# Regrouping the opening phase of a two-layer GLA and pooling kernel: stages of two tiles that carry keys and half of the values, each half of a modulation as one run

## The chip, the cores and the metric

The kernel runs on one core of one Trainium2 chip. The metric is the device time of one execution in microseconds (us), lower is better. Engines are named as in the profile: PE is TensorE's matmul side and PEld its weight load, DVE is VectorE, ACT is ScalarE, POOL is GpSimd, SP is the queue from which most transfers are started.

## What is computed

One batch of 256 rows of width 2048 (`x`) passes through two layers; 256 more rows (`ctx`) serve the first layer only. All tensors are float32.

```
for i in 0, 1:
    sh, sc, gt = split(silu(c) @ w_ada[i] + b_ada[i], 3)          # the modulation
    u = x * (1 + sc) + sh
    layer 0: uc = ctx * (1 + sc_c) + sh_c                         # same weights, condition c_ctx
             k, v, rf, rb of uc -> two final states s_f, s_b      # w_in_e columns of keys, values, ranks
             h = u @ w_in_e                                       # keys, values, ranks, queries, gates, convolution inputs
             y = concat(gla(h, s_f, s_b) * silu(gate), conv(h)) @ w_out_e
    layer 1: h = u @ w_in_o;  y = (pool(h) * silu(gate)) @ w_out_o
    x = layer_norm(alpha * x + gt * y, ln_g[i], ln_b[i])
```

The change concerns only the start of layer 0: the modulation's shift and scale for `x` and `ctx`, the modulated inputs `u` and `uc`, and their products with the key and value columns of `w_in_e`.

## The kernel before

**Products.** A float32 product is done as three matmuls in the type fp32r: both operands are split into a rounded part h and a rest l, and `mm3` issues uh*wh, uh*wl and ul*wh (L190 to L192), 512 columns each. A weight unit arrives in a `raw` buffer (four buffers of 1 MB, `load_unit`, L138, from the SP queue); `split_unit` makes the parts: a copy on ACT (L152), a subtraction on DVE (L153). The buffer is free when both are done. The list `specs` holds the weight units in the order of use, `w_ahead(nl, ns)` loads up to nl and splits up to ns units from the one in use on, `w_next` hands out the next.

**Opening phase.** The contraction of 2048 is cut into 16 tiles of 128. A stage takes one or two of them (`STAGES`: 1, 1, then seven times 2). `stage_u` makes the modulated input of its tiles. `mod_rows` loads the modulation weights of these columns, first the scale half, then the shift half, in units of 1 MB: for two tiles two units a half, for one tile one. Each unit is used by 8 or 16 products in four column strips of the array (L274, tile `ada`; float32 shows as two instructions a product), all into one bank `ps`. `to_cols` copies the bank (`arow`, ACT, L285) and turns it to columns (`adaT`, L288); `add_bias` finishes scale and shift (`modT`). Then the input tiles are transposed (`px`, L390 and L391), scaled on ACT and DVE (`u`), and split (`uxh`, `uxl` for `x`, `uch`, `ucl` for `ctx`). After every fourth tile four products in four strips add to the ranks (`pr`, L406, two instructions each).

`stage_k` multiplies a stage's tiles with the two halves of the key columns: for each half four groups (two row blocks of `x`, two of `ctx`) of 3 matmuls a tile, so 24 matmuls for two tiles; each group's bank is added to `knat` on DVE (L426; the first stage copies on ACT). `v_fill` does the same for one half of the value columns (tile `vfill`, added to `vnat`). `FILLS` places it for tiles 0 to 7 only. What is left of the values, tiles 8 to 15 of the first half and all of the second, is done behind the opening phase by `gemm` in quads of four tiles (tile `vacc`), after the keys are transposed (`nT`).

**Order.** The program text calls `stage_u` of a stage ahead of `stage_k` of the stage before it. A planner at build time then fixes each engine's order: an instruction with a lower priority number (by default its place in the text; `prio` shifts it) goes first when its inputs are there by the planner's own estimates. `issue_after` makes instructions of a block follow a given one on their engine. Engines run their order strictly, and `raw` buffers are given out in the order of the text.

**Background.** The other modulation columns are worked off on DVE, in units of 1 MB that are also `raw` buffers (`ada_accum`, L534, four instructions of 128x512 a unit). `pump_ada` starts them: none in the opening phase, then three per quad of values (`ADA_V`), and fewer later. The GLA's gate and score work is started by a budget at the same ticks, of 4500 a quad of values and 3000 a quad later.

Of the kernel before, what the change touches and what calls it, by code (L numbers as in the profile page):

```python
# [2 lines left out]

# [6 lines left out]
F32 = mybir.dt.float32  # L10
# [3 lines left out]
ALU = mybir.AluOpType  # L14
# [3 lines left out]
P = 128  # L18
D = 2048
KT = D // P  # L20
# [9 lines left out]
UF_ACT = 1  # L30
KRAW = False
GW_AT = 12
ADA_0 = {}
ADA_ORDER = "cgh"
ADA_O = 1
ADA_PRIO = 0
# [17 lines left out]
B_X = 3000  # L54
LA_SPLIT = 1
JG = 4
STAGES = (1, 1, 2, 2, 2, 2, 2, 2, 2)


@with_exitstack  # L60
def kernel(
# [47 lines left out]
    def const(shape, dt, name):  # L109
        return cpool.tile(shape, dt, tag=name, name=name)  # L110
# [77 lines left out]
    def mm3(acc, u, w, start, stop):  # L188
        (uh, ul), (wh, wl) = u, w
        nc.tensor.matmul(out=acc, lhsT=uh, rhs=wh, start=start, stop=False)  # L190
        nc.tensor.matmul(out=acc, lhsT=uh, rhs=wl, start=False, stop=False)  # L191
        nc.tensor.matmul(out=acc, lhsT=ul, rhs=wh, start=False, stop=stop)  # L192


    rows0 = slot([32, P], F32, "rows0")
# [29 lines left out]
    nc.gpsimd.dma_start(rows2[8:24, :], as_rows(pool_scale[0]))  # L225
    nc.gpsimd.dma_start(rows2[24:26, :], as_rows(gla_norm_w[0]))

    sel4 = const([P, 4], F32, "sel4")
    nc.vector.tensor_reduce(out=sel4, in_=ident.rearrange("p (g v) -> p v g", g=4)[:, 0:4, :], axis=AX.X, op=ALU.add)

# [29 lines left out]
    nc.gpsimd.dma_start(wr, w_in_e[0][:, D : D + 32].rearrange("(k p) n -> p k n", p=P))  # L260


    def mod_rows(k0, n):

        nw = n * P
        ps = mp([P, nw], "ada")
        nk = 2048 // nw
        for half, c0 in ((0, D + k0 * P), (1, k0 * P)):
            for kk in range(0, KT, nk):
                r = load_unit(w_ada[0], kk, nk, c0, nw)  # L270
                for j in range(nk):
                    kt = kk + j
                    g = kt % 4
                    nc.tensor.matmul(  # L274
                        out=ps[32 * g : 32 * g + 32, :], lhsT=sil[:, kt, 2 - 2 * half : 34 - 2 * half], rhs=r[:, j, :],
                        start=half == 0 and kt < 4, stop=half == 1 and kt >= KT - 4,
                    )
        return ps

    arow_ins = []  # L280

    def to_cols(ps, nw):
        n = nw // P
# [79 lines left out]

    quad_u = []

    def stage_u(k0, n):
        w, n0 = n * P, k0 * P
        xc = xcs.pop(k0, None)
        if xc is None:
            xc = load_xc(k0, n)  # L370
        xs, cs = xc[:, 0:2, :], xc[:, 2:4, :]
        ps = mod_rows(k0, n)
        if k0 == 0:
            cols_0()
        if k0 == 4:
            cols_1()
        if k0 == GW_AT:
            gate_weights()
        pt = to_cols(ps, w)
        ks = slice(k0, k0 + n)  # L380
        add_bias(scT[:, ks, :], pt[:, :, 0:2], bT[0][:, 16 + k0 : 16 + k0 + n].unsqueeze(2).to_broadcast([P, n, 2]), True)
        add_bias(shT[:, ks, :], pt[:, :, 2:4], bT[0][:, ks].unsqueeze(2).to_broadcast([P, n, 2]), False)
        for j in range(n):
            kt = k0 + j
            if kt % 2 == 0:
                quad_u.append(slot([P, 2, 512], F32, "u"))
            u = quad_u[-1]
            px = mp([P, 512], "px")
            for t in range(2):
                nc.tensor.transpose(out=px[:, t * P : (t + 1) * P], in_=xs[:, t, j * P : (j + 1) * P], identity=ident)  # L390
                nc.tensor.transpose(out=px[:, 256 + t * P : 256 + (t + 1) * P], in_=cs[:, t, j * P : (j + 1) * P], identity=ident)  # L391
# [7 lines left out]
            nc.scalar.copy(uch[q][:, i, :], uc)  # L399
            nc.vector.tensor_tensor(out=uxl[q][:, i, :], in0=ux, in1=uxh[q][:, i, :].bitcast(F32), op=ALU.subtract)  # L400
            nc.vector.tensor_tensor(out=ucl[q][:, i, :], in0=uc, in1=uch[q][:, i, :].bitcast(F32), op=ALU.subtract)
            if i == 3:
                pr = mp([P, 512], "pr")
                for g in range(4):
                    kk = kt - 3 + g
                    nc.tensor.matmul(  # L406
                        out=pr[32 * g : 32 * g + 32, :], lhsT=wr[:, kk, :], rhs=quad_u[kk // 2][:, kk % 2, :],
                        start=True, stop=True,
                    )
                if q == 0:  # L410
                    nc.vector.tensor_copy(r_acc, pr)
                else:
                    nc.vector.tensor_tensor(out=r_acc, in0=pr, in1=r_acc, op=ALU.add)

    def stage_k(k0, n):
        for nb in range(2):
            parts = w_next((W_E, k0, n, nb * 512), 0, 0)
            for m in range(4):
                acc = acc_bank("kacc")
                for j in range(n):  # L420
                    mm3(acc, utile(m, k0 + j), parts[j], j == 0, j == n - 1)
# [18 lines left out]

    vnat = []

    def v_fill(nb, kt, nk):

        parts = w_next((W_E, kt, nk, 1024 + nb * 512), 0, 0)
        if not vnat:
# [1 line left out]
        with prio(FILL_PRIO):  # L448
            for m in range(4):
                acc = acc_bank("vfill")  # L450
                for j in range(nk):
                    mm3(acc, utile(m, kt + j), parts[j], j == 0, j == nk - 1)
# [110 lines left out]
    }  # L563
    ada_bg.extend(jobs[n]() for n in ADA_ORDER)

    prev, k0 = None, 0
    for n in STAGES:
        if prev:
            w_ahead(2, SPLIT_0)
        stage_u(k0, n)  # L570
        if prev:
            stage_k(*prev)
            pump_ada(ADA_0.get(sum(prev), 0))
            for f in FILLS.get(sum(prev), ()):
                v_fill(*f)
        elif SPLIT_0:
            with tc.issue_after(arow_ins[0].ins):
                w_ahead(2, 2)
        prev = (k0, n)
        k0 += n  # L580
    n0_done[0] = True
    w_ahead(4, 2)
    stage_k(*prev)


    bg = []
# [801 lines left out]
```

## Time and profile before

| | us |
|---|---|
| Median of 3 runs (lowest, highest) | 1006.15 (1005.88, 1007.38) |
| Profiled execution, its own time | 1010.29 |
| Profiled execution, span of the trace | 1008.5 |
| First matmul of the keys starts (from the span's start) | 17.09 |
| Last `nT` transposes done, first `vacc` matmul starts | 198.91 |

The profile describes one execution. An engine's busy time is the time in which it had an instruction, a wait is the idle time ahead of an instruction with what ended it. Matmuls overlap, so the pace of PE is read from the distance of two starts and not from the duration of one matmul.

### The profile page before, as it was taken

To read this page: it belongs to the slowest core of one execution; us is meant where nothing else is said; L and a number is where in the kernel's file an instruction comes from. 1 tells how busy PE (TensorE), PEld (TensorE's weight loads), DVE (VectorE), ACT (ScalarE), POOL (GpSimd) and SP (SyncE) were. 2 spreads that over 40 slices of the span, in tenths; PEclk is the share of its full clock that TensorE was granted. 3 is DMA by queue.
4 is the path that set the end of the run, shared out by engine and by line. 5 is a ranking of instruction groups with operands and counts; after the bars stand their busy time and mean duration, and the time that the engine had idled before them with its cause. 6 is when DMAs were issued, how large, how long until landed. Compare 5 with 4: busy or idle time off the path is not lost.

```text
span 1008.5 us, 14323 instructions
## 1 busy us (share of the span) xinstructions
PE 960.9 (95%) x5654; PEld 759.2 (75%) x5654; DVE 801.6 (79%) x1142; ACT 469.3 (47%) x643; POOL 24.4 (2%) x56
## 2 busy tenths in 40 slices
PE   5899999999999999999999899999999999989995
PEld 4566656778878877887878778888778778778885
DVE  1555546979996999779999688897979997666676
ACT  2422214356675676236454344445745555435340
POOL 2000000000000000000000000000010001000000
PEclk9999999999999999999999999999999999999998
DMA  9977889566787586867767877985497999875532
GB/s 265 329 263 262 276 284 336 193 243 231 258 302 252 188 269 219 257 206 274 241 228 234 284 255 247 353 298 207 152 368 275 304 334 322 278 266 203 174 119 83
DMA packets 150371, 255.44 MB, mean 253 GB/s; under 512 B 5078, under 2 KB 46720, under 8 KB 150304
## 3 DMA queue, kind: packets, MB, share of 16 engines
q1 hardware_dynamic: 146592, 245.13, 72.4%
q0 software_dynamic: 2896, 8.72, 2.7%
q10 hardware_dynamic: 816, 0.68, 0.3%
q8 instruction: 44, 0.72, 0.3%
q14 instruction: 23, 0.19, 0.0%
HBM read 252.41 MB, written 2.10 MB: 252 GB/s over the span
## 4 chain that ended last, share of the span: by engine, by line
PE 41%; DVE 33%; DMA 18%; issue 5%; ACT 3%; SPq 0%; DVEq 0%; ACTq 0%
DMA raw<-in_w_ada_dram 15%; DVE wl L153 11%; DVE aacc L534 9%; PE oacc L191 5%; PE oacc L192 5%; PE oacc L190 5%; DMA raw<-in_w_in_o_dram 3%; PE xacc L192 3%; PE xacc L191 3%; PE xacc L190 3%; PE ada L274 2%; PE kacc L190 2%; PE kacc L192 2%; PE kacc L191 2%; PE pr L406 1%
## 5 line engine op out<-in xcount | busy, mean ns | idle before, releaser
L152 ACT CAST wh<-raw 128x1024 fp32r<-128x1024 f32 (+1 forms) x250 | 257.0, 1044 | 252.6 <-PE xacc L192 77.9
L153 DVE TENSOR_TENSOR wl<-raw,wh 128x1024 fp32r<-128x1024 f32 (+1 forms) x250 | 297.3, 1210 | 49.3 <-ACT wh L152 47.1
L534 DVE SCALAR_TENSOR_TENSOR aacc<-raw,sil,aacc 128x512 f32<-128x512 f32 x240 | 179.0, 747 | 34.2 <-DMA raw<-in_w_ada_dram 30.7
L190 PE MATMUL xacc<-wh,uxh 128*128 128x512 f32 x384 | 153.8, 400 | 0.0
L191 PE MATMUL xacc<-wl,uxh 128*128 128x512 f32 x384 | 150.9, 393 | 0.9 <-DVE wl L153 0.9
L192 PE MATMUL xacc<-wh,uxl 128*128 128x512 f32 x384 | 151.1, 394 | 0.0
L191 PEld LDWEIGHTS xacc<-wl,uxh 128*128 128x128 f32 x384 | 72.6, 189 | 17.3 <-DVE wl L153 1.7
L190 PEld LDWEIGHTS xacc<-wh,uxh 128*128 128x128 f32 x384 | 72.5, 189 | 15.6 <-issue 0.5
L192 PEld LDWEIGHTS xacc<-wh,uxl 128*128 128x128 f32 x384 | 72.4, 188 | 15.6 <-issue 0.2
L426 DVE TENSOR_TENSOR knat<-kacc,knat 128x512 f32<-128x512 f32 x64 | 42.8, 685 | 35.8 <-PE kacc L192 35.6
L285 ACT COPY arow<-ada 128x256 f32<-128x256 f32 (+1 forms) x9 | 3.1, 349 | 101.9 <-PE ada L274 101.9
L274 PE MATMUL ada<-raw,sil 128*32 128x256 f32 (+1 forms) x576 | 36.2, 380 | 12.0 <-DMA raw<-in_w_ada_dram 12.0
L190 PE MATMUL xacc<-wh,u1h 128*128 128x512 f32 x112 | 44.8, 400 | 0.8 <-ACT u1h L1167 0.8
L190 PE MATMUL oacc<-wh,y1h 128*128 128x512 f32 (+1 forms) x120 | 45.5, 379 | 0.0
L192 PE MATMUL oacc<-wh,y1l 128*128 128x512 f32 (+1 forms) x120 | 45.0, 375 | 0.0
L191 PE MATMUL oacc<-wl,y1h 128*128 128x512 f32 (+1 forms) x120 | 45.0, 375 | 0.0
L191 PE MATMUL xacc<-wl,u1h 128*128 128x512 f32 x112 | 44.1, 394 | 0.3 <-DVE wl L153 0.3
L192 PE MATMUL xacc<-wh,u1l 128*128 128x512 f32 x112 | 44.0, 393 | 0.0
L274 PEld LDWEIGHTS ada<-raw,sil 128*32 128x32 f32 x576 | 17.0, 118 | 28.6 <-issue 12.3
L190 PE MATMUL kacc<-wh,uxh 128*128 128x512 f32 x64 | 26.8, 418 | 1.5 <-ACT uxh L398 1.5
L1228 PE MATMUL xacc<-wh,dm 128*128 128x512 f32 x64 | 26.2, 409 | 1.6 <-ACT wh L152 1.6
L190 PE MATMUL kacc<-wh,uch 128*128 128x512 f32 x64 | 26.4, 412 | 0.5 <-DVE knat L426 0.5
(339 smaller groups left out, 1865.0 us busy)
## 6 DMA issues: line engine op xcount, KB each, us to landing
raw<-in_w_ada_dram SPq DMA_DIRECT2D x96, 1024.0 KB, 6.3
raw<-in_w_in_e_dram SPq DMA_DIRECT2D x54, 1024.0 KB, 6.0
raw<-in_w_in_o_dram SPq DMA_DIRECT2D x32, 1024.0 KB, 7.1
raw<-in_w_out_e_dram SPq DMA_DIRECT2D x16, 1024.0 KB, 6.7
raw<-in_w_out_o_dram SPq DMA_DIRECT2D x16, 1024.0 KB, 5.1
raw<-in_w_in_e_dram SPq DMA_DIRECT2D x18, 512.0 KB, 7.2
raw<-in_w_pool_dram SPq DMA_DIRECT2D x4, 1024.0 KB, 7.5
gt<-in_b_ada_dram POOLq DMA_DIRECT2D x8, 256.0 KB, 3.8
```

The source lines that it names most:

```text
L152: nc.scalar.copy(h, r[:, j : j + w, :])
L153: nc.vector.tensor_tensor(out=l, in0=r[:, j : j + w, :], in1=h.bitcast(F32), op=ALU.subtract)
L190: nc.tensor.matmul(out=acc, lhsT=uh, rhs=wh, start=start, stop=False)
L191: nc.tensor.matmul(out=acc, lhsT=uh, rhs=wl, start=False, stop=False)
L192: nc.tensor.matmul(out=acc, lhsT=ul, rhs=wh, start=False, stop=stop)
L274: nc.tensor.matmul(out=ps[32 * g : 32 * g + 32, :], lhsT=sil[:, kt, 2 - 2 * half : 34 - 2 * half], rhs=r[:, j, :], start=half == 0 and kt ...
L285: arow_ins.append(nc.scalar.copy(a[:, :nw], ps))
L406: nc.tensor.matmul(out=pr[32 * g : 32 * g + 32, :], lhsT=wr[:, kk, :], rhs=quad_u[kk // 2][:, kk % 2, :], start=True, stop=True,)
L426: nc.vector.tensor_tensor(out=dst, in0=acc, in1=dst, op=ALU.add)
L534: e.scalar_tensor_tensor(out=a, in0=r[j], scalar=sc, in1=a, op0=ALU.mult, op1=ALU.add)
L1228: nc.tensor.matmul(out=accs[0], lhsT=dh, rhs=wh, start=f, stop=False)
```

## The change

Eight stages of two tiles take the place of nine. In each, `stage_k` is followed by `v_fill` of the same two tiles for the first half of the values, so that all 16 tiles of that half are done in the opening phase and the `gemm` of it is skipped. From the fifth stage on each stage also starts one background unit. The text now has `stage_k` of a stage ahead of `stage_u` of the next one, and `stage_u` has a priority of 2000 less, so it goes first wherever it may.

The scale half of the next modulation may not go ahead of the fourth group of the current stage, the shift half not ahead of the eighth (`PLACE`). The products of a half follow each other as one run; from the second stage on the unit that is loaded last is used first. The input's transposes follow the shift half's products. Both key units of the next stage are loaded between the scale half's and the shift half's units; in the first stage the first key unit is loaded and split ahead of the modulation's last unit. In later stages the first key unit is split right behind the copy `arow`, the second behind the input's last copy. The rank products follow the sixth group of a stage, together. `keep_warm` adds matmuls on zeros whose result nobody reads: 7 behind the first transpose, 5 behind each scale unit of the first stage.

```
-ADA_0 = {}
+ADA_0 = {i: 1 for i in range(4, 8)}
-FILLS = {2: [(0, 0, 2)], 4: [(0, 2, 2)], 6: [(0, 4, 2)], 8: [(0, 6, 2)]}
+FILLS = {k + 2: [(0, k, 2)] for k in range(0, KT, 2)}
+PLACE = (3, 7)
+STAGE_PRIO = 2000
+WARM = (7, 5)
-STAGES = (1, 1, 2, 2, 2, 2, 2, 2, 2)
+STAGES = (2, 2, 2, 2, 2, 2, 2, 2)
...
+    def keep_warm(n, behind=None):
+        idle = mp([P, 256], "idle")
+        for _ in range(n):
+            with tc.issue_after(behind.ins) if behind else nullcontext():
+                nc.tensor.matmul(out=idle, lhsT=zero[:, 0:P], rhs=zero, start=True, stop=True)
...
     nc.tensor.transpose(out=pc, in_=crow, identity=ident[:32, :32])
+    keep_warm(WARM[0])
...
-    def mod_rows(k0, n):
+    def mod_rows(k0, n, behind, between):
...
         for half, c0 in ((0, D + k0 * P), (1, k0 * P)):
+            rs = []
             for kk in range(0, KT, nk):
-                r = load_unit(w_ada[0], kk, nk, c0, nw)
...
+                if k0 == 0 and half and kk:
+                    w_ahead(1, 1)
+                elif k0 and half and not kk:
+                    w_load(min(len(specs), wst["u"] + 2))
+                rs.append((kk, load_unit(w_ada[0], kk, nk, c0, nw)))
+
+            order = [(kk, kk + j, r[:, j, :]) for kk, r in (reversed(rs) if k0 else rs) for j in range(nk)]
+            first = None
+            for i, (kk, kt, w) in enumerate(order):
+                g = kt % 4
+                with behind(half) if first is None or not k0 else tc.issue_after(first.ins):
+                    ins = nc.tensor.matmul(
...
+                first = first or ins
+                if (i + 1) % nk == 0:
+                    between(half, i + 1, ins)
...
-    def stage_u(k0, n):
+    def stage_u(k0, n, groups):
...
+        def between(half, k, ins):
+            if (half, k) == (1, KT // 2 if k0 == 0 else KT):
+                with tc.issue_after(ins.ins):
+                    for j in range(n):
+                        transposes(j)
+                    if k0 == 0:
+                        cols_0()
+            if k0 == 0 and half == 0:
+                keep_warm(WARM[1], ins)
+
+        def behind(unit):
+            if not groups:
+                return nullcontext()
+            return tc.issue_after(groups[PLACE[unit]].ins)
...
         pt = to_cols(ps, w)
+        if k0:
+            with tc.issue_after(arow_ins[-1].ins):
+                w_ahead(1, 1)
...
+    def ranks(kt, behind):
...
+        with tc.issue_after(behind.ins), prio(-2 * STAGE_PRIO):
+            first = product(3)
+            with tc.issue_after(first.ins):
+                for g in range(3):
+                    product(g)
...
-    prev, k0 = None, 0
-    for n in STAGES:
-        if prev:
-            w_ahead(2, SPLIT_0)
-        stage_u(k0, n)
-        if prev:
-            stage_k(*prev)
-            pump_ada(ADA_0.get(sum(prev), 0))
-            for f in FILLS.get(sum(prev), ()):
-                v_fill(*f)
...
+    starts = [sum(STAGES[:i]) for i in range(len(STAGES))]
+    groups = []
+    for i, (k0, n) in enumerate(zip(starts, STAGES)):
+        if i == 0:
+            stage_u(k0, n, [])
+            with tc.issue_after(h_ins[-1].ins):
+                w_ahead(3, 2)
+        if i + 1 < len(STAGES):
+            xcs[k0 + n] = load_xc(k0 + n, STAGES[i + 1])
+        groups = []
+        stage_k(k0, n, groups)
+        for f in FILLS.get(k0 + n, ()):
+            v_fill(*f, groups)
+        pump_ada(ADA_0.get(i, 0))
+        if i + 1 < len(STAGES):
+            with prio(-STAGE_PRIO):
+                stage_u(k0 + n, STAGES[i + 1], groups)
+                with tc.issue_after(h_ins[-1].ins):
+                    w_ahead(3, 2)
...
     for nb in range(2):
+        if not V_Q[nb]:
+            continue
```

## Rows read from the trace of the kernel before

**Rows 1.** Busy time of each engine over the span, its share, instructions (the page).
```profile
PE 960.9 (95%) x5654; PEld 759.2 (75%) x5654; DVE 801.6 (79%) x1142; ACT 469.3 (47%) x643; POOL 24.4 (2%) x56
```
**Rows 2.** Opening phase by windows: stretch, length, engines' busy us, granted clock, DMA share, GB/s.
```profile
17.09:198.91 181.82, 175.59 (x1148) 117.41 (x1149) 108.37 (x195) 53.39 (x98) 0.41 (x2) 1.00 0.86 277
```
**Rows 3.** Waits of PE in that stretch, total us, times, longest.
```profile
PE ada L274 <- DMA raw<-in_w_ada_dram: 4.6, 4, 1.8
```
**Rows 4.** The first 30 us by windows, columns as in rows 2.
```profile
0.00:10.00 10.00, 2.22 (x33) 1.69 (x33) 1.10 (x6) 1.48 (x2) 6.88 (x17) 1.00 0.86 221
10.00:20.00 10.00, 6.63 (x46) 5.04 (x47) 2.92 (x8) 3.04 (x7) 0.16 (x1) 1.00 1.14 276
20.00:30.00 10.00, 9.55 (x96) 6.75 (x95) 2.35 (x6) 6.39 (x14) 0.00 (x0) 1.00 1.10 338
```
**Rows 5.** Timeline of the start: start us, us, engine, line, operation.
```profile
7.67 1.93 PE L274 MATMUL ada<-raw,sil 128*32 128x128 f32 x32 [4.86 <-DMA raw<-in_w_ada_dram]
...
12.14 1.94 PE L274 MATMUL ada<-raw,sil 128*32 128x128 f32 x32 [2.54 <-DMA raw<-in_w_ada_dram]
...
17.09 0.80 PE L190 MATMUL kacc<-wh,uxh 128*128 128x512 f32 x1 [1.09 <-ACT uxh L398]
...
18.11 0.63 PE L190 MATMUL kacc<-wh,uxh 128*128 128x512 f32 x1
...
18.54 0.63 PE L191 MATMUL kacc<-wl,uxh 128*128 128x512 f32 x1
...
22.57 0.40 PE L190 MATMUL kacc<-wh,uch 128*128 128x512 f32 x1
...
22.80 0.39 PE L191 MATMUL kacc<-wl,uch 128*128 128x512 f32 x1
```
**Rows 6.** Timeline of PE in the last stage before, around modulation runs.
```profile
162.27 0.39 PE L192 MATMUL kacc<-wh,ucl 128*128 128x512 f32 x1
162.59 1.93 PE L274 MATMUL ada<-raw,sil 128*32 128x256 f32 x32
164.45 0.50 PE L190 MATMUL kacc<-wh,uxh 128*128 128x512 f32 x1
164.79 0.40 PE L191 MATMUL kacc<-wl,uxh 128*128 128x512 f32 x1
...
166.16 1.07 PE L274 MATMUL ada<-raw,sil 128*32 128x256 f32 x16 [0.74 <-DMA raw<-in_w_ada_dram]
167.16 0.50 PE L192 MATMUL kacc<-wh,uxl 128*128 128x512 f32 x1
```
**Rows 7.** Timeline of PE, first of three pieces of one quad's ranks.
```profile
86.72 1.05 PE L406 MATMUL pr<-u,wr_acc 128*32 128x512 f32 x4
87.70 0.50 PE L190 MATMUL kacc<-wh,uxh 128*128 128x512 f32 x1
88.04 0.40 PE L191 MATMUL kacc<-wl,uxh 128*128 128x512 f32 x1
88.36 1.04 PE L406 MATMUL pr<-u,wr_acc 128*32 128x512 f32 x2
```
**Rows 8.** Transfers from 60 to 200 us: count, size, median us to landing.
```profile
raw<-in_w_ada_dram SPq DMA_DIRECT2D x23, 1024.0 KB, 7.1
raw<-in_w_in_e_dram SPq DMA_DIRECT2D x12, 512.0 KB, 7.4
raw<-in_w_in_e_dram SPq DMA_DIRECT2D x4, 1024.0 KB, 8.7
```
**Rows 9.** All transfers into `raw` from 60 to 200 us, issue to landing.
```profile
DMA to landing us min/median/max: 5.2/7.4/10.4
```
**Rows 10.** Costliest groups (the page): DVE's background units.
```profile
L534 DVE SCALAR_TENSOR_TENSOR aacc<-raw,sil,aacc 128x512 f32<-128x512 f32 x240 | 179.0, 747 | 34.2 <-DMA raw<-in_w_ada_dram 30.7
```
**Rows 11.** Timeline of PE behind the opening phase.
```profile
581.29 0.99 PE L974 MATMUL yT<-ident,y 128*128 128x128 f32 x4 [5.14 <-DVE y L966]
```
**Rows 12.** Timeline of DVE at that place.
```profile
580.00 0.75 DVE L534 SCALAR_TENSOR_TENSOR aacc<-raw,sil,aacc 128x512 f32<-128x512 f32 x1 [5.58 <-DMA raw<-in_w_ada_dram]
```

More of the change, by code (lines that the diff above doesn't have):

```diff
@@ L1 @@
 import math
-from contextlib import ExitStack, contextmanager
+from contextlib import ExitStack, contextmanager, nullcontext
 import concourse.bass as bass
@@ L191, in mm3 @@
         nc.tensor.matmul(out=acc, lhsT=uh, rhs=wl, start=False, stop=False)
-        nc.tensor.matmul(out=acc, lhsT=ul, rhs=wh, start=False, stop=stop)
+        return nc.tensor.matmul(out=acc, lhsT=ul, rhs=wh, start=False, stop=stop)
     rows0 = slot([32, P], F32, "rows0")
@@ L268, in mod_rows @@
         for half, c0 in ((0, D + k0 * P), (1, k0 * P)):
+            rs = []
             for kk in range(0, KT, nk):
-                r = load_unit(w_ada[0], kk, nk, c0, nw)
[L271 to L276, printed above, removed]
-                    )
+                if k0 == 0 and half and kk:
[9 more added lines that the diff above has]
+                    ins = nc.tensor.matmul(
+                        out=ps[32 * g : 32 * g + 32, :], lhsT=sil[:, kt, 2 - 2 * half : 34 - 2 * half], rhs=w,
+                        start=half == 0 and i < 4, stop=half == 1 and i >= KT - 4,
+                    )
+                first = first or ins
+                if (i + 1) % nk == 0:
+                    between(half, i + 1, ins)
         return ps
-    arow_ins = []
+    arow_ins, h_ins = [], []
     def to_cols(ps, nw):
@@ L371, in stage_u, with transposes @@
         xs, cs = xc[:, 0:2, :], xc[:, 2:4, :]
-        ps = mod_rows(k0, n)
-        if k0 == 0:
-            cols_0()
+        pxs = {}
+        def transposes(j):
+            pxs[j] = mp([P, 512], "px")
+            for t in range(2):
+                nc.tensor.transpose(out=pxs[j][:, t * P : (t + 1) * P], in_=xs[:, t, j * P : (j + 1) * P], identity=ident)
+                nc.tensor.transpose(out=pxs[j][:, 256 + t * P : 256 + (t + 1) * P], in_=cs[:, t, j * P : (j + 1) * P], identity=ident)
+        def between(half, k, ins):
[11 more added lines that the diff above has]
+            return tc.issue_after(groups[PLACE[unit]].ins)
+        ps = mod_rows(k0, n, behind, between)
         if k0 == 4:
@@ L387, in stage_u @@
             u = quad_u[-1]
[L388 to L391, printed above, removed]
+            px = pxs[j]
             ux, uc = u[:, kt % 2, 0:256], u[:, kt % 2, 256:512]
@@ L402, in stage_u, with product, stage_k @@
             if i == 3:
[L403 to L415, printed above, removed]
+                ranks_due.append(kt)
+    ranks_due = []
+    def ranks(kt, behind):
+        pr = mp([P, 512], "pr")
+        def product(g):
+            kk = kt - 3 + g
+            return nc.tensor.matmul(
+                out=pr[32 * g : 32 * g + 32, :], lhsT=wr[:, kk, :], rhs=quad_u[kk // 2][:, kk % 2, :], start=True, stop=True)
+        with tc.issue_after(behind.ins), prio(-2 * STAGE_PRIO):
[3 more added lines that the diff above has]
+                    product(g)
+        if kt == 3:
+            nc.vector.tensor_copy(r_acc, pr)
+        else:
+            nc.vector.tensor_tensor(out=r_acc, in0=pr, in1=r_acc, op=ALU.add)
+    def stage_k(k0, n, groups):
         for nb in range(2):
@@ L420, in stage_k @@
                 for j in range(n):
-                    mm3(acc, utile(m, k0 + j), parts[j], j == 0, j == n - 1)
+                    ins = mm3(acc, utile(m, k0 + j), parts[j], j == 0, j == n - 1)
+                groups.append(ins)
+                if ranks_due and (nb, m) == (1, 1):
+                    ranks(ranks_due.pop(), ins)
                 dst = knat[m][:, nb * 512 : (nb + 1) * 512]
@@ L441, with v_fill @@
     vnat = []
-    def v_fill(nb, kt, nk):
+    def v_fill(nb, kt, nk, groups):
         parts = w_next((W_E, kt, nk, 1024 + nb * 512), 0, 0)
```

13 lines of the change are left out of this document (5 added, 8 removed).

## Prediction

> **What bounds the kernel now.** I read four views. The page's busy times first: PE is busy 95% of the span, DVE 79% [rows 1], so the end is set by PE's work, its pace, and its idle time. Then the windows: in the opening phase, from the first key matmul at 17.09 to the first `vacc` matmul at 198.91, PE is busy 175.6 of 181.8 us, DVE 108.4 [rows 2]. PE has 6.2 us of idle time there, 4.6 of them waits for modulation units [rows 3]. So the phase is one of PE's work with small transfer waits, and DVE has 73 us to spare. Before it stand 17.09 us in which PE waits for the first input [rows 5]. The timelines give prices: how far starts lie apart on PE, and what a change of work costs. I work on the stretch from 0 to the end of the first half's values; all behind it keeps its matmuls.
>
> **Prices.** A key matmul in a steady run starts 0.23 us after the last one [rows 5]. Around a modulation run the distances are 0.32 and 0.34 [rows 6], so an interruption costs 0.2 more than its work. A run of two units takes 1.86 from its start to the next one's, a run of one unit 1.00 [rows 6].
>
> **The first stage: +5.8.** Before, two units of 1 MB go ahead of the first key matmul, the second lands at 12.14, and the keys start 17.09−14.08 = 3.0 us behind the end of its products [rows 5]. Now four units of 1 MB (4.2 million bytes), one key unit (0.5), 0.5 of input and about 0.4 of small tensors on the other queues must land: 5.6. Before, the windows moved 2.2 by 10 us and 5.0 by 20 [rows 4], so 5.6 is there at 20 + 0.6/0.338 = 21.9 at that pace. The pace dipped when the buffers were taken; at an even 0.33 from 10 us on it is 20.3, and the small tensors partly come later. The buffer of the last unit is that of the first, free at about 10 us, so it doesn't bind. I take 19.5 for the landing, 1.0 for its products, 2.4 for the way to the first key matmul (3.0 less about 0.6, since the transposes now stand ahead of the copy): 22.9, bounds 20.9 and 26. The warm-up matmuls stand in time that PE waits anyway; without that cover their 17 would cost some 0.4 to 0.9 each by the pace of a modulation product, 7 to 15 us.
>
> **One stage less: −3.4.** The separate second stage's two modulation runs (1.4 and 1.0), its column matmuls and transposes (0.65) and two interruptions fall away; all key matmuls stay.
>
> **Modulation in one run: −3.9.** Two separate units cost 2×(1.00+0.2) = 2.4, a pair 1.86+0.2 = 2.05 [rows 6]: 0.35 saved a pair. Before, 5 of 14 pairs stood together; one of the other units was cut in two, 0.75 more. So 9×0.35+0.75.
>
> **Ranks together: −8.5.** Before, the four products of a quad came in pieces. A piece with two products takes as long as one with one, 1.0 [rows 7], since they use different strips of the array. There are ten pieces in the phase, two of them of double length, hence 11.5 + 10×0.2 = 13.5 us. Four in one run should take 1.0 to 1.05, as the 8 products of a modulation unit over four strips take 1.07 [rows 6]: 4×1.25 = 5.0. If only two strips ran side by side, 4×0.98 more: bound −4.6.
>
> **Clock: −1.8.** The first key matmuls start 0.43 us apart, later ones 0.23 [rows 5], the distances of 512 columns at 1.2 and near 2.4 GHz, though the granted clock stands at 1.00 [rows 4]; PE had been idle for most of the first 12 us. Some nine matmuls ran so: 1.8 us. With matmuls in the waits they should run at the higher level; bounds 0 and −1.8. The Trainium skill, TensorE: Matmul & The Clock Gate (Why this matters for your kernels), says that the engine drops to half its clock when left idle and that activity brings it back. The spacing agrees; by that rule the idle stretch ahead of the last unit, where no extra matmul stands, could undo the gain, and this term would be 0.
>
> **Waits inside the phase: +3.8.** This term decides. The shift half's two units need the buffers of the scale half's: there are four, and two hold the next stage's keys until they are split behind `arow` and behind the input's last copy. So the shift units go out only when the scale run ends, and behind the key loads on SP. They land 7.1 us later by the median [rows 8]. In between stand 24 key matmuls, 5.45 us, and in three stages of seven 1.25 of ranks. That leaves 1.65 in four stages and 0.4 in three: 7.9. In the fifth to seventh a background unit takes a buffer as well; I add 0.7 each, 2.1. Together 10 us of idle time in place of 6.2. Behind PE's waiting matmul stand all other matmuls, above all the eighth to twelfth group. Bounds: 0, if the planner puts the twelve value groups' 5.45 us into the wait; 20, if every unit takes 8.7, the longest median here [rows 8], and a background unit costs its whole 3 us. The next stage's input chain (copy, columns, scaling, split, about 5 us with the key's split) stays under transposes and value matmuls, 6.9 us.
>
> A key or value unit of half the size takes as long to land, 7.4 against 7.1 [rows 8]. Tiles 8 to 15 of the values now come in four such units, not two of 1 MB: 4×7.4−2×8.7 = 12 us more of buffer time, over four buffers 3 us if these bound the phase. I leave it in the bound. The Trainium skill, DMA: Bandwidth & Descriptors (Measured), asks for at least 1 MiB a transfer; this case's row agrees, and by the rule alone I would add those 3 us.
>
> **Hidden.** DVE gets four background units earlier (16×0.747 = 12 us [rows 10]) and, net, four more bank additions (under 3 us), against 73 free us. Without that cover they would cost 15. The zero fill and the skipped `gemm` cost nothing on PE.
>
> **Behind the phase: 0, bounds −6 and +6.** Two quads of values are fewer, so two background units and 9000 of the gate budget move later, under matmuls. DVE has the room, but which unit it waits on changes. Before, one such order costs 5.1 us: the `yT` transposes wait for DVE, which waits for a transfer [rows 11, 12]. It may vanish or come up elsewhere.
>
> **Sum.** 5.8−3.4−3.9−8.5−1.8+3.8 = −8.0. The profiled execution took 1010.29 us, 1.8 of it outside the span; it becomes 1002.3. The median lies 4.1 below that execution: 998.2. A difference under 0.2% (2 us) can't be told from none: 1004.1 to 1008.2 is "same".
>
> **Rivals.**
> 1. *The shift half comes late (slower).* One mechanism: four buffers, two held by keys. At the longest landing seen, 10.4 [rows 9], the seven waits are 4×4.95+3×3.7 = 31 us, 21 more than I took: 1019. It decides at 18 us of waits, 1.1 more a stage. For it: transfers moved 277 GB/s in this phase with PE short of data at times [rows 2, 3], and now some 54 million bytes must land by about 177 us, 305 GB/s. Against: 338 GB/s was reached [rows 4], and the value groups may fill a wait. Chance 0.17.
> 2. *The start gives it back (no change).* First key matmul at 26, clock gain 0, ranks only −4.6: 3.1+1.8+3.9 = 8.8 worse, 1007. For it: twice the bytes ahead of the first product. Against: the bytes wait for the same queue in both kernels. Chance 0.11.
> 3. *More than forecast.* The value groups fill the waits (10 less 4) and the `yT` wait goes: 998.2−6−5 = 987. For it: a planner that puts other work ahead; against: the fixed places. Chance 0.20.
> 4. *The forecast*, 991 to 1004: chance 0.52.
>
> Faster: 0.52+0.20 = 0.72; same 0.11; slower 0.17. With one in ten cut on each side the range is 986 to 1010: below it lies the best of case 3 (all bounds together 980), above it most of rival 1.
>
> **What would show it.** First key matmul at 21 to 26 us; its neighbours 0.23 apart; modulation runs of 32 instructions, two a stage, each under 2.1; ranks in four runs of about 1.05; stages 22.5 to 25 us apart; waits of PE for modulation units about 10 us in all, at the shift half; first `vacc` (second half) at about 213 against 220.7 for the same point before (198.91 and 96 matmuls). The forecast is wrong if these waits pass 18 us, if the values' additions or splits on DVE hold the next stage's keys, or if PE's waits behind the phase differ by more than 6 us.

## The result and the profile after

The changed kernel takes 1033.95 us (median of 4 runs, 1029.83 to 1036.91), the kernel before beside it 1006.01: a ratio of 1.027, 95% interval 1.023 to 1.031. That is slower by 27.9 us, outside the predicted range and 15 us beyond the rival that ends on the slow side. In the profiled executions the span grew from 1008.5 to 1035.1 us, by 26.6.

The page of the changed kernel, busy times over the span (before: [rows 1]):

```profile
PE 969.2 (94%) x5624; PEld 776.8 (75%) x5624; DVE 805.8 (78%) x1143; ACT 469.5 (45%) x640; POOL 24.4 (2%) x56
```

Thirty instructions fewer on PE, and yet 8.3 us more of busy time, as well as more idle time. The busy time lies ahead of the first key matmul: 17.5 us there against 5.9, with modulation products for two tiles and the matmuls of zeros, in time that PE waits anyway. The idle time lies in the phase behind it. Windows of the changed kernel: the phase, the first keys, and three later stretches (columns as in [rows 2]; the three numbers at the end are the granted clock, the DMA share and GB/s). The phase runs from the first key matmul to 242.40: the first half's values end where the first `nT` starts, at 238.78, and 3.6 us stand for the 32 `nT` transposes that come there before the change (now 16 do, and 16 later):

```profile
25.58:242.40 216.82, 192.80 (x1167) 142.31 (x1168) 124.30 (x203) 54.54 (x93) 0.41 (x2) 0.93 0.78 250
20.00:30.00 10.00, 6.51 (x32) 4.86 (x33) 4.43 (x11) 4.14 (x9) 0.00 (x0) 0.66 0.83 257
50.00:60.00 10.00, 8.11 (x29) 6.31 (x28) 6.74 (x12) 4.61 (x9) 0.00 (x0) 0.83 0.91 294
140.00:160.00 20.00, 15.37 (x83) 11.48 (x82) 8.43 (x17) 5.55 (x10) 0.00 (x0) 0.83 0.77 247
180.00:200.00 20.00, 15.34 (x75) 10.64 (x76) 11.80 (x19) 6.49 (x11) 0.00 (x0) 0.67 0.72 228
```

PE idles 24.0 us here, against 6.2 before [rows 2]; the transfers move 250 GB/s where they moved 277; the granted clock is 0.93 where it was 1.00. So the phase became slower with all three engines and the queue less used: they wait for each other more.

Waits of PE in that stretch up to the first `nT` at 238.78, total us, times, longest (before: [rows 3]):

```profile
PE ada L296 <- DMA raw<-in_w_ada_dram: 13.7, 8, 5.9
PE kacc L193 <- ACT uxh L445: 10.8, 7, 1.9
PE kacc L195 <- DVE uxl L447: 1.1, 1, 1.1
```

Two kinds: a modulation run waits for its unit (11.7 us ahead of shift runs, 2.1 ahead of scale runs), and the first key matmul of six later stages waits for `uxh`, the end of the input's chain (1.67 of that row is the first stage's). The second kind had 1.5 us in all before, 1.1 of it in the first stage:

```profile
PE kacc L190 <- ACT uxh L398: 1.5, 2, 1.1
```

The start (timeline of PE; before: [rows 5]):

```profile
21.32 1.07 PE L296 MATMUL ada<-raw,sil 128*32 128x256 f32 x16 [2.01 <-DMA raw<-in_w_ada_dram]
22.89 1.02 PE L313 MATMUL adaT<-sel,arow 128*128 128x4 f32 x4 [0.49 <-ACT arow L310]
25.58 0.79 PE L193 MATMUL kacc<-wh,uxh 128*128 128x512 f32 x1 [1.67 <-ACT uxh L445]
26.17 0.63 PE L194 MATMUL kacc<-wl,uxh 128*128 128x512 f32 x1
26.60 0.63 PE L193 MATMUL kacc<-wh,uxh 128*128 128x512 f32 x1
```

The first key comes 8.5 us later than before, and its neighbours are still 0.43 apart.

One stage in full, the seventh, with the longest wait. Its scale run ends at 167.6. Timeline of SP's queue in the changed kernel:

```profile
166.84 0.88 SPq L141 DMA_DIRECT2D raw<-in_w_in_e_dram  x2
167.82 1.43 SPq L141 DMA_DIRECT2D raw<-in_w_ada_dram  x2
```

What all queues moved there, from 163 to 182 us in 40 equal slices of 0.475 us:

```profile
GB/s 379 358 308 364 358 259 17 0 0 0 69 65 229 388 388 354 401 375 429 356 246 321 220 175 194 248 349 347 347 347 347 347 351 380 125 24 22 13 22 9
```

Windows of the same kernel around it, columns as above:

```profile
169.00:173.00 4.00, 4.00 (x20) 3.29 (x19) 2.08 (x3) 0.00 (x0) 0.00 (x0) 1.00 1.05 362
177.00:182.00 5.00, 0.27 (x4) 0.20 (x8) 1.91 (x2) 0.17 (x1) 0.00 (x0) 0.74 0.61 173
182.00:186.00 4.00, 4.00 (x36) 1.86 (x29) 0.00 (x0) 0.57 (x2) 0.00 (x0) 0.50 0.27 53
```

And the chain of waits there (start, us, what):

```profile
166.03 1.22 DVE swl L156
167.25 0.16 issue
167.40 0.91 DVE wg L494
168.31 0.56 DVE aacc L596
168.87 0.02 issue
168.89 12.80 DMA raw<-in_w_ada_dram
181.68 0.04 issue
181.73 3.68 PE ada L296 x32
```

To be read in this order: all four buffers are held, two by the scale units, one by a value unit and one by a background unit, so nothing is moved from 166.3 on (0 GB/s in three slices) until they are given back; then four transfers, 3 MB, go out within 2.1 us, the two key units first; the queue moves 362 GB/s, but the last modulation unit, whose buffer a background unit held until 168.87, lands 12.8 us after its issue, at 181.7. The median for such a unit was 7.1 before, the longest 10.4 [rows 8, 9]. Not all of the 12.8 is the burst's size: 3.1 million bytes at 362 GB/s would take 8.7 us, an estimate. The slices show some 200 GB/s from 173.5 to 175, and from 179.6 to the landing under 25 GB/s. What made this slow end no run shows. This stage is also the only one that loads the gate weights: a memset of them, 0.91 us, stands on DVE ahead of the background unit's last instruction, and six transfers of 64 KB on ACT's queue land beside the units. In the other six stages the last unit took 7.4 to 9.6 us.

The shift run then starts 16.0 us behind the scale run's start, at half the clock (0.50): 3.64 us instead of 1.93. In the other stages from the second on, shift runs start 9.4 to 12.6 behind the scale runs.

The clock, at the second stage's seam (timeline of PE):

```profile
49.90 0.39 PE L195 MATMUL vfill<-swh,ucl 128*128 128x512 f32 x1
52.18 0.50 PE L193 MATMUL kacc<-wh,uxh 128*128 128x512 f32 x1 [1.89 <-ACT uxh L445]
...
52.98 0.53 PE L194 MATMUL kacc<-wl,uxh 128*128 128x512 f32 x1
53.30 0.63 PE L195 MATMUL kacc<-wh,uxl 128*128 128x512 f32 x1
53.73 0.63 PE L193 MATMUL kacc<-wh,uxh 128*128 128x512 f32 x1
```

After 1.89 us of idle time the starts go from 0.23 to 0.43 apart for some 3 us: the lower of the two levels. This follows four of the six waits at the seams, not those of 1.56 us at 79.3 and 0.70 at 125.7. From the first key to the first `nT`, 38 key matmuls start so, each 0.2 us longer than at the upper level: 7.6 us lost. Before there were 7, with 1.4.

The ranks (timeline of PE; pieces before: [rows 7]):

```profile
62.18 1.08 PE L460 MATMUL pr<-u,wr_acc 128*32 128x512 f32 x8
63.06 1.92 PE L296 MATMUL ada<-raw,sil 128*32 128x256 f32 x32
```

### The profile page after: what moved, and what is told of

It reads as the page before. It is cut to its first block, busy times and chain, and to the rows that moved or that the text cites. A ratio compares the mean times of both kernels' runs of the same rounds, so it can differ in the third digit from the quotient of the medians.

```text
span 1035.1 us, 14252 instructions
## 1 busy us (share of the span) xinstructions
PE 969.2 (94%) x5624; PEld 776.8 (75%) x5624; DVE 805.8 (78%) x1143; ACT 469.5 (45%) x640; POOL 24.4 (2%) x56
## 4 chain that ended last, share of the span: by engine, by line
PE 43%; DVE 30%; DMA 18%; issue 5%; ACT 3%; SPq 0%; DVEq 0%; ACTq 0%
DMA raw<-in_w_ada_dram 16%; DVE wl L156 11%; DVE aacc L596 7%; PE oacc L194 5%; PE oacc L195 5%; PE oacc L193 5%; PE ada L296 3%; PE kacc L195 2%; PE kacc L193 2%; PE xacc L195 2%; PE xacc L193 2%; PE xacc L194 2%; PE kacc L194 2%; ACT wh L155 1%; DMA raw<-in_w_in_e_dram 1%
## 5 line engine op out<-in xcount | busy, mean ns | idle before, releaser
L155 ACT CAST wh<-raw 128x1024 fp32r<-128x1024 f32 x244 | 253.7, 1053 | 242.6 <-PE xacc L195 74.8
L156 DVE TENSOR_TENSOR wl<-raw,wh 128x1024 fp32r<-128x1024 f32 x244 | 294.3, 1222 | 72.6 <-ACT wh L155 70.3
L487 DVE TENSOR_TENSOR knat<-kacc,knat 128x512 f32<-128x512 f32 x56 | 38.0, 690 | 23.6 <-PE kacc L195 23.2
L310 ACT COPY arow<-ada 128x256 f32<-128x256 f32 x8 | 3.0, 373 | 112.4 <-PE ada L296 112.4
L296 PE MATMUL ada<-raw,sil 128*32 128x256 f32 x512 | 33.8, 404 | 17.1 <-DMA raw<-in_w_ada_dram 17.1
L195 PE MATMUL kacc<-wh,uxl 128*128 128x512 f32 x64 | 28.2, 457 | 1.2 <-DVE uxl L447 1.1
## 6 DMA issues: line engine op xcount, KB each, us to landing
raw<-in_w_ada_dram SPq DMA_DIRECT2D x96, 1024.0 KB, 6.3
raw<-in_w_in_e_dram SPq DMA_DIRECT2D x52, 1024.0 KB, 5.6
raw<-in_w_in_o_dram SPq DMA_DIRECT2D x32, 1024.0 KB, 7.1
raw<-in_w_out_e_dram SPq DMA_DIRECT2D x16, 1024.0 KB, 6.5
raw<-in_w_out_o_dram SPq DMA_DIRECT2D x16, 1024.0 KB, 5.1
raw<-in_w_pool_dram SPq DMA_DIRECT2D x4, 1024.0 KB, 7.9
```

Source lines behind the costliest of these rows:

```text
L155: nc.scalar.copy(h, r[:, j : j + w, :])
L156: nc.vector.tensor_tensor(out=l, in0=r[:, j : j + w, :], in1=h.bitcast(F32), op=ALU.subtract)
L195: return nc.tensor.matmul(out=acc, lhsT=ul, rhs=wh, start=False, stop=stop)
L296: ins = nc.tensor.matmul(out=ps[32 * g : 32 * g + 32, :], lhsT=sil[:, kt, 2 - 2 * half : 34 - 2 * half], rhs=w, start=half == 0 and i < 4, ...
L310: arow_ins.append(nc.scalar.copy(a[:, :nw], ps))
```

## The experiments

**Theory A**: the keys of the next stage, loaded ahead of the shift half, hold two of four buffers and go first on the queue; the shift unit lands late, the planner moves value matmuls into that gap, and the chain at the seam (the step from one stage's last matmul to the next stage's first key) loses its cover. **Rival B**: the background units cost it. **Rival C**: the clock, falling behind short waits, is a cost of its own. **Rival D**: the late first stage, or the 16 value tiles in the phase, cost it in any order. Ratios are against the kernel before on the same chip, whose medians there were 1008 to 1010 us; single executions of it spread from 1003 to 1014, so a profiled phase is compared by its rows, a whole by its interval.

"Phase end" is the first `nT`. Where eight groups of values stand behind it, as before, 96×0.2275 = 21.8 us are added: 195.3+21.8 = 217.1 before, 238.8 after.

**The background units** (changed kernel):

```diff
-ADA_0 = {i: 1 for i in range(4, 8)}
+ADA_0 = {}
```

> The changed kernel (1034 us) without the four background units of its opening phase. Theory A (the four raw buffers limit the phase; a background unit holds one until DVE has used it): the waits for modulation units in the sixth to eighth stage (2.9, 5.9, 1.0 and 1.6 us) fall below 3 us together, and most of the slow matmuls behind them go: 1020 to 1026 us. Theory B (the written places and the priority put the shift run late whatever the loads do): the units only move behind the phase, 1031 to 1037 us.

1025.7 us, ratio 1.017 (1.013 to 1.021). Phase end 224.5, 14.3 earlier; waits for modulation units in the phase 6.3, of them 3.4 at the seventh stage's shift run. Of those 14 us some 10 reach the whole; the rest is paid behind the phase, as the units are made later: PE waits 5.0 for `dm`, where it had waited 1.8, and 3.2 ahead of `xT`. So B holds in the phase for a good part, and is no way out.

**Key and value units in slots of another pool** (changed kernel):

```diff
-KRAW = False
+KRAW = True
```

> The changed kernel with the key and value units of the opening phase in buffers of another pool, so that the four raw buffers serve the modulation (and four background units) alone. Theory A: the shift half's units go out before the scale run ends; PE's waits for modulation units in the phase fall from 13.7 us behind the first keys to under 4, fewer value groups stand ahead of the shift run, the wait for the first split input (9.1 us in seven places) falls to under 4, and with them most of the slow matmuls: 1003 to 1015 us. Theory B: still above 1028 us.

1024.0, ratio 1.016 (1.012 to 1.019). PE's largest waits over the span in this run:

```profile
PE kacc L193 <- ACT uxh L445: 10.6, 2, 9.0
PE kacc L193 <- ACT wh L155: 7.1, 2, 4.1
```

No wait for a modulation unit of 0.2 us or more is left in the phase, with the same loads in the text's order: what made the units late was the buffers, not the queue. Yet the time fits neither expectation. Now the keys themselves are late (`wh`), and one wait of 9.0 stands in the seventh stage, whose chain goes back to the gate weights: their last transfer starts at 172.1 and takes 6.3, and ACT takes up the input behind it. The waits moved.

**No warm-up** (changed kernel):

```diff
-WARM = (7, 5)
+WARM = (0, 0)
```

> The changed kernel without the 17 added matmuls on zeros. If they do nothing for the clock where it counts (the first nine key matmuls of the changed kernel start 0.43 us apart all the same): within 2 us of 1034. If they hold the clock up for the first stage: some 2 to 3 us slower, with the columns and transposes of the first stage at half pace. If they hold up the first modulation products, whose run starts at 8.88, just when the seven end: 1 us faster.

1031.1, ratio 1.022 (1.018 to 1.026), its interval overlapping that of the change itself; first key at 26.25, 0.7 later. The extra matmuls did hold the clock up for a while: the products of the shift half's first unit take 1.07 us with them and 1.93 without. But the first keys start 0.43 apart in both, behind waits of 1.4, 2.0 and 1.67 us in the changed kernel, and in the whole nothing can be told.

**The key loads behind the shift units** (changed kernel without these lines; the next loads' own line then issues them):

```diff
-                elif k0 and half and not kk:
-                    w_load(min(len(specs), wst["u"] + 2))
```

> The changed kernel without the load of the next stage's two key units ahead of the shift half's: they come behind it. Theory A: one shift unit finds a buffer before the scale run ends, the shift run comes earlier and the waits shrink by a third to a half: 1015 to 1026 us, unless the keys now come too late. Theory B: 1031 to 1037 us.

1014.2 (10 runs), ratio 1.005 (1.003 to 1.007) against the change's 1.027: some 22 us are back by two lines. Phase end 212.7; but 21 value matmuls, 4.8 us, stand behind it there, so 217.5. Waits up to 217 in this run:

```profile
PE kacc L193 <- ACT uxh L443: 7.4, 3, 3.8
PE kacc L195 <- DVE uxl L445: 1.5, 1, 1.5
PE ada L294 <- DMA raw<-in_w_ada_dram: 1.2, 3, 0.5
```

The last stage's two runs, timeline of PE in this run:

```profile
185.48 1.93 PE L294 MATMUL ada<-raw,sil 128*32 128x256 f32 x32
...
191.55 0.39 PE L194 MATMUL vfill<-swl,uxh 128*128 128x512 f32 x1
192.28 1.93 PE L294 MATMUL ada<-raw,sil 128*32 128x256 f32 x32 [0.34 <-DMA raw<-in_w_ada_dram]
```

6.8 us from run to run, where the changed kernel has 12.6 in that stage; 9.2 in the stage shown above, where it has 16.0. Of 24 value matmuls 8 to 24 stay behind the shift run, where 0 to 10 did. Transfers of 1 MB into `raw` land in 6.2 us by the median (7.0 after), and the queue moves 279 GB/s where it moved 244 (both from 60 us on, to 200 and 220). A holds. Of the waits for the input's chain most of what is left, 3.8 and 1.5, stands in the seventh stage. The first key is at 27.7, so D's late start is still in the 1014.

**Both** (key loads behind, no background units):

> The changed kernel with both of: the next stage's key units loaded behind the shift half's (1014 us by itself) and no background units in the opening phase (1026 us by itself). Theory A, by which both free buffers in the same cycle: gains add up in part, 1005 to 1011 us. If the background units only hurt where keys hold the buffers: 1012 to 1017.

1014.8 (10 runs), ratio 1.007 (1.003 to 1.010): nothing more than the key loads alone. The background units hurt only where the keys hold the buffers.

**The clock, first try** (changed kernel; three matmuls of zeros behind the value groups, issued from the program's text there):

```diff
+        if i + 1 < len(STAGES):
+            keep_warm(3, groups[-1])
```

> The changed kernel with three more matmuls on zeros (about 1.5 us) behind the last value group of each stage but the last, where PE waits 1.4 to 1.9 us for the first split input. If the fall of the clock behind these waits is a cost of its own: the 38 key and value matmuls that start 0.43 us apart become fewer than 18, 4 to 6 us faster than the changed kernel (1034). If the clock falls by the modulation waits all the same: within 2 us. If the zeros stand in the way of other work: 3 us or more slower.

1098.4, ratio 1.089 (1.085 to 1.093). It missed its question: the bank for the zeros is taken ahead of the bank for the next modulation, so that no scale run could start until the value groups were through. Waits of PE over the span:

```profile
PE ada L296 <- DMA raw<-in_w_ada_dram: 52.4, 10, 8.3
```

It shows the price of a shift half with little to cover it, 6.4 to 8.3 us a stage.

**The clock, second try** (the same matmuls, taken behind the columns of the next stage, so that they stand at the seam):

```diff
+        if groups:
+            keep_warm(3, groups[-1])
```

> The changed kernel with three matmuls of zeros into a spare bank at the stage's seam, behind the last value matmul that stands there, where PE waited 1.4 to 1.9 us for the next keys. In the changed kernel the granted clock was 0.83 and 0.67 behind such waits and 38 key and value matmuls started 0.43 apart. Theory (the fall of the clock behind a short wait is a cost of its own): fewer than 25 such gaps, 1029 to 1032 us. Rival (the clock falls behind the waits for transfers, which stay, and the three matmuls only take time): 35 to 40 gaps, 1033 to 1037 us.

1036.9, ratio 1.028 (1.024 to 1.032): no gain. The seam in this run (timeline of PE), and its clock by windows:

```profile
50.43 1.46 PE L239 MATMUL idle<-zero 128*128 128x256 f32 x6
52.48 0.50 PE L193 MATMUL kacc<-wh,uxh 128*128 128x512 f32 x1 [0.59 <-ACT uxh L447]
52.82 0.40 PE L194 MATMUL kacc<-wl,uxh 128*128 128x512 f32 x1
```

```profile
50.00:60.00 10.00, 9.41 (x42) 7.54 (x41) 7.58 (x13) 4.62 (x9) 0.00 (x0) 1.00 0.93 294
```

The clock stays up there (1.00 against 0.83), and slow starts fall from 38 to 13, 5 us saved. Yet the phase ends at 239.5, 0.7 later. The zeros take 7×1.46 = 10.2 us, where 6.8 of waits for `uxh` went, the waits for modulation units grow by 3.9, and three shift runs instead of two run at the lower level. So C found no gain in this form. As the zeros cost 3.4 more than the waits that they fill, the run doesn't show what a clock held at no cost would be worth.

**The ranks alone** (kernel before, with the four products of a quad in one run, by the change's own function):

> The kernel before with the rank products of a quad in one run behind the sixth key group of the stage that holds the quad's last tile; all else as before. By the prediction's term: 8.5 us faster than the kernel before (bound 4.6). Rival: the pieces stood where PE would have waited for transfers, so that these waits grow by what the ranks save: under 3 us faster.

1003.0 (10 runs), ratio 0.995 (0.992 to 0.997); phase end 8.1 earlier, of which some 5 us (3 to 8) show in the whole. This part of the change is sound, and the kernel with it alone beats both.

**The ranks and a first stage of two tiles** (kernel before):

```diff
-STAGES = (1, 1, 2, 2, 2, 2, 2, 2, 2)
+STAGES = (2, 2, 2, 2, 2, 2, 2, 2)
```

> The kernel before with the ranks in one run and its first two stages of one tile joined to one of two; the separate runs of its modulation, the twelve value groups and its order of loads stay. Against the run with the ranks alone (0.9948 of before): theory (the first stage's price as measured in the changed kernel, 8.5 later, less the 3.4 of a stage saved): first key at 24 to 26 us, 4 to 6 us slower than the ranks alone, 1007 to 1009. Rival (the price as forecast, 5.8 less 3.4): first key at 22 to 23, 1004 to 1006. Second rival (a larger first stage gives back nothing, since the second stage's runs stood under waits anyway): 1011 or more.

1000.1 (10 runs), ratio 0.993 (0.991 to 0.996). Between the profiles the phase ends 4.2 later than with the ranks alone, as the theory said, with the first key at 26.3; the whole is not slower, against all three expectations. The intervals overlap, so that in the whole no cost of the first stage is shown here; D's first half falls or is small.

**All 16 value tiles in the phase** (kernel before, with the lines that fill the last stage and leave out the empty `gemm`):

```diff
-FILLS = {2: [(0, 0, 2)], 4: [(0, 2, 2)], 6: [(0, 4, 2)], 8: [(0, 6, 2)]}
+FILLS = {k + 2: [(0, k, 2)] for k in range(0, 16, 2)}
```

> The kernel before with all 16 tiles of the values' first half in the opening phase, eight units of half the size in place of four of them and two of full size; stages, order and priorities as before. Theory A (buffers limit the phase): the value units hold buffers in the last four stages too, but the 22 us of value matmuls give the transfers time: within 3 us of the kernel before. Rival: more units of half size cost some 3 us or more each four: 3 to 8 us slower. Should the moved matmuls cover the waits behind 100 us (2.8 us): 2 to 4 us faster.

1023.1, ratio 1.015 (1.011 to 1.019), slower than any of the three expectations. The phase ends at 219.1, only 2.0 behind the same point before. The other 12 come later; waits of PE in this run:

```profile
PE xacc L1232 <- ACT dm L1188: 5.0, 1, 5.0
...
PE xT L1163 <- issue: 3.2, 1, 3.2
PE oacc L190 <- ACT swh L152: 3.0, 1, 3.0
```

Two groups of values fewer start six background units less, and by these waits they are caught up at the layer's end, where PE stands still for them. This is read from the waits, and no run of this kernel with more units a tick shows it. The change itself starts four units earlier against that; its share is seen next. Of D's second half 2 us in the phase are left, and the background behind it.

**One more background unit in each tick of the value phase** (key loads behind the shift units, and):

```diff
-ADA_V = 3
+ADA_V = 4
```

> The changed kernel with the keys' units behind the shift units again (1014 us measured), and one more background unit in each tick of the value phase, which gives back the units that two fewer value groups no longer start. Theory (4 to 5 us behind the phase are background units that come late and are caught up at the layer's end): 1009 to 1012 us, and the waits of PE for the gate columns go from 2.5 to under 1 us. Rival (DVE, which makes these products, has no more room there and its values come later): 1014 to 1019 us.

1008.6 (10 runs), ratio 1.001 (0.998 to 1.003), some 4.4 us less than without; the wait for the gate columns, 2.5 us in the changed kernel and 1.9 with the keys later, is 0.8. The two intervals just touch. So the background accounts for about what the account below has behind the phase.

**The first stage cut in two again** (key loads behind the shift units, and):

```diff
-STAGES = (2, 2, 2, 2, 2, 2, 2, 2)
+STAGES = (1, 1, 2, 2, 2, 2, 2, 2, 2)
-            if (half, k) == (1, KT // 2 if k0 == 0 else KT):
+            if (half, k) == (1, KT // 2 if k0 == 0 and n > 1 else KT):
```

with `ADA_0` one stage later, for the same places.

> The changed kernel with the keys' units behind the shift units again (1014 us measured), and its first stage cut into two of one tile as in the kernel before. Theory (of what is left, the first stage's late start costs 8.5 and saves 3.4): first key at 17 to 20 us, 1008 to 1011 us. Rival (the second stage's own shift half waits for its transfer uncovered, as no value matmuls stand there yet, and the gain goes into that wait): first key at 17 to 20 us, waits of PE for modulation units 3 us or more ahead of the third stage, 1013 to 1017 us.

1012.5 (10 runs), ratio 1.003 (1.000 to 1.005). The first key comes at 16.8, 10.9 earlier, and the phase ends only 3.8 earlier; the whole gains about 2, between the two expectations and within the intervals.

**All three**:

> The changed kernel with three of its parts undone or made good at once: the keys' units behind the shift units, the first stage cut into two of one tile, and one more background unit in each tick of the value phase. With the first and the third alone it took 1008.6 us, with the first and second 1012.5. Theory (the three causes add up, and the first stage is worth the 2 to 4 us that the phases showed): 1004.5 to 1006.5 us. Rival (the late background units and the late start share their cover, so that undoing the one leaves nothing for the other): 1008 to 1010 us. Second rival (nothing but the three stood against the ranks' gain): 1003 us, the time of the kernel before with the ranks in one run.

1007.6 (12 runs), ratio 0.997 (0.995 to 0.999). Against 1.005, 1.001 and 1.003 for the parts, they add up about as the theory said (−0.0044 and −0.0024 make 0.998); in us the time lies 1.1 above the theory's range, with the kernel before 1.1 slower beside it than in the two runs that the range came from. To the 0.995 of the ranks alone 0.25% remain, about half the width of either interval, and these overlap: whether half-sized units, the fixed places or nothing is behind them stays open.

## Why the prediction was wrong

The account to the end of the first half's values, 242.4 after (238.78 and the 32 transposes) against 220.75 before (198.91 and 96 matmuls), by the prediction's terms:

```
term                     forecast   measured
first stage                 +5.8       +8.5
one stage less              -3.4       (taken as forecast)
modulation in one run       -3.9       (taken as forecast)
ranks together              -8.5       -8.1 (ranks alone)
clock                       -1.8      +10.3  (worked out below)
waits inside the phase      +3.8      +17.8  (24.0 idle less 6.2)
sum                         -8.0      +21.2
phase as measured                     +21.7
behind the phase             0         +4.9
```

0.5 us of the phase have no name.

**Waits inside the phase: the step that failed.** The prediction put 10 us here, all of it at the shift half, and nothing at the input's chain, which was to stay "under transposes and value matmuls". Measured are 24.0: 13.7 for units and 10.2 for that chain, 9.1 at six seams and `uxl` 1.1. So the sentence on the chain is what failed most. Its cover was spent twice: the term's lower bound lets the value groups fill the wait for the units, and the sentence has them cover the chain. The planner put 14 to 24 of 24 ahead of the shift run, and the chain lost its cover.

The mechanism of the units was read rightly: four buffers, shift units that go out only when the scale run ends, and behind the key loads. The prediction said that this term decides, and rival 1 names this part of what happened. That 13.7 came near the 10 is luck, two errors against each other. The landing was taken as the median of transfers as they stood before, 7.1; the last unit of a stage took 9.5 by the median, six of seven under the old longest of 10.4 and one 12.8. In the stage shown the wait itself empties the queue, and then four transfers go out at once. The value groups ahead of the shift run made up for most of that. The background unit's buffer, priced at 0.7 a stage, is what released the last unit in the seventh. Nor do the recorded bounds add up: 8.7 for every unit gives 4×3.25+3×2.0 = 19, and three background units at 3 us make it 28, not 20. The 24.0 lie under that, under the 31 of rival 1, and beyond the 18 at which it decides. And the sign that was set, unit waits past 18 us, did not appear; the loss stood at a wait that had no price.

Taking the two lines away brings back 22 us and cuts the distance from run to run, 16.0 to 9.2 in the worst stage, and the unit waits from 13.7 to 1.2; giving keys and values buffers elsewhere removes the unit waits and makes the keys late instead. This is shown, not argued.

**Clock: the sign was wrong.** Forecast as a gain of 0 to 1.8, it was a loss: 6.2 for slow key matmuls (7.6 less 1.4), some 2.5 for two modulation runs at 2.68 and 3.64 instead of 1.93, and 1.6 for the transposes and columns behind these two, which start 0.21 apart in place of 0.11. The bounds looked only at the first keys, not at what the forecast's own new waits would do to the clock. With the clock held at the seams by zeros nothing was gained. The prediction's sentence that the rule of the Trainium skill, TensorE: Matmul & The Clock Gate (Why this matters for your kernels), could make the first term 0 was right: from 20 to 30 us the granted clock was 0.66, and the first keys stood 0.43 apart behind the waits of 1.4, 2.0 and 1.67 us. At the second stage's seam a single idle stretch of 1.89 us was followed by the lower level.

**First stage: the mechanism right, the size off.** 25.58 against 22.9, within its bounds of 20.9 to 26. The last unit's products start at 21.32, so it landed 1.8 later than taken, and the way to the first key took 3.2 from the end of its products against 2.4. Less the stage that it saves, 3.8 to 4.2 of it is left at the phase's end by two runs, and about 2 or nothing in the whole.

**Right.** The ranks, to 0.4 us in the phase, though only some 5 of the 8.1 show in the whole. Twelve of the fourteen modulation runs of 32 at 1.86 to 1.93, and a run of 8 ranks at 1.08. Behind the phase, 0 with bounds of ±6, came to +4.9, by the cause it named, background units that move, as the run with one more unit a tick bears out. The term left in the bound, that key and value units of half the size take as long to land, did not come: their median from 60 to 220 us is 4.0 us in the changed kernel against 7.4 for 512 KB before [rows 8], though most of these went out first, with little in flight, so that the two rows don't compare the sizes alone. The rule of the Trainium skill, DMA: Bandwidth & Descriptors (Measured), that asks for 1 MiB had no price in these rows that could be seen.

Stages were forecast 22.5 to 25 us apart; their first keys stand 22.8 to 34.7 apart, the last three the farthest.

## What to carry to other kernels

Where a pool of buffers is the bound, a load that is moved ahead pays with the landing of the next load that shares the pool; don't price it by the landing times of the old order, since a wait that empties the queue sends everything at once behind it, and here the last of the burst set the time. Give each stretch of covering work to one wait only: count what must be hidden between two points against what there is, for all claimants together. A part that is sound by itself (here the ranks) should be timed by itself; it may be the only one to keep.

## What the runs showed of the hardware

The clock fell to its lower level behind four of five waits of 1.4 to 1.9 us at the seams (0.83 in 50 to 60; the 0.67 in 180 to 200 also holds what followed a wait of 5.9). It did not behind the one of 1.56 at 79.3, so the length of a wait alone does not tell it here. At the second seam it was back after some 3 us of matmuls, and six instructions of zeros in that wait (1.46 us) kept it at 1.00. Of the 5 us won in pace by such zeros nothing reached the phase's end.

The queue's pace rose to 362 GB/s with four transfers in flight, and still the last of them took 12.8 us for 1 MB, 1.8 times the median, with under 25 GB/s moved in its last 2 us. Over the seven stages the last modulation unit took 7.4 to 12.8 us from its issue.
